# Second layer of a decoder trunk: a projection's weight splits tied behind the softmax scalings, and the last output rows' splits placed ahead of the begun rows' low parts

## The chip, the cores and the metric

The kernel runs on one core of a Trainium2 chip. The metric is the device time of one execution in microseconds (us), and the median of several runs is compared. The engines of a core work side by side, each through its own queue in order: TensorE (PE in the profile, with its weight loads as PEld), VectorE (DVE), ScalarE (ACT), GpSimd (POOL), and SyncE (SP), which here only issues DMA transfers.

## The reference

The model is a trunk of two layers over 512 tokens of width 1024, in float32. Only the second layer matters here. Before it, the first layer (a gated-DeltaNet mixer) and its feed-forward part have left the residual `x`. The second layer computes

```python
h = rms_norm(x, ln_mix[1])
proj = h @ swa_w_q                       # 12 query heads of 64, and 4 memory heads of 64
q = apply_partial_rope(proj[..., :768])
mix_out = sliding_window_attention(q, shared_k, shared_v, swa_sinks)   # window 128, 2 KV heads
mem_o = memory_attention(proj[..., 768:], mem_k, mem_v)                # 256 memory tokens
x = x + concatenate([mix_out, mem_o]) @ w_out[1]
x = x + swiglu(rms_norm(x, ln_ffn[1]), w_gate_up[1], w_down[1])
```

and the shared keys and values come from the normed `x` through `w_kv`. A final RMS norm follows.

## The kernel before, in words

Activations lie transposed: 128 channels on the partitions, 512 tokens along the free axis, so `x` is eight tiles `x[0..7]` of 128 x 512. Matrix products are made in a reduced format (fp32r) with a correction. Every operand is split in two: a high part, which is the value rounded to that format, and a low part, the rest. A product of a weight tile with an activation tile is three matmuls (`mm3`, L191): high times high, high times low, low times high. So a weight block of 128 x 1024 (one output tile of a projection, eight input tiles) costs 24 matmuls, and before them one split (`weight`, L180, with `split`, L166): an ACT copy `whi<-wraw` (L138) and a DVE subtraction `wlo<-wraw,whi` (L151). The raw block comes by one DMA of 512 KB (`load`, L174) into one of two `wraw` buffers. There are three pairs of `whi`/`wlo`, and two further pairs `oh`/`ol` for two output rows.

The attention part is `swa` (L1147). The queries are eight projections `queries(t)`: t = 0 to 5 are pairs of window heads, 6 and 7 the memory heads. For each tile t there follow

- `score(t)`: 16 matmuls into the PSUM tag `qk`, and DVE instructions that add the band mask and take the maxima (L751);
- `softmax(t)`: exponentials on ACT (L788), the denominators and their reciprocal on DVE (`den`, L793, L794), and the scaling of the exponentials by the reciprocal (`scale`, L799): for the token blocks n = 0 and 2 two instructions each on DVE (L806), for n = 1 and 3 two each on ACT (L804);
- `weighed(t)`: for each n, transposes of the scaled tile on PE into the PSUM tag `pt` (two banks), a copy out to `pf` (ACT L840, for n = 3 DVE L838), and then the products with the values, again into a `pt` bank;
- `settle(t)`: the result is split out of that bank into a high part (ACT, `h<-pt`) and a low part (DVE, `l<-pt,h`, L1213). The low part is kept behind the scaling that came last.

The tiles are taken in the order 6, 7, 0, 1, 2, 3, 4, 5. The loop at L1238 has steps t = 0 to 5: step t scores tile t, weighs the tile (6, 7, 0, 1, 2, 3)[t], softmaxes the tile (7, 0, 1, 2, 3, 4)[t], and in between, as PE work that needs nothing of these, runs the projection `queries(t + 2)` for t under 4 and the first four of eight input tiles of output row 0 or 1 for t = 4 and 5. After the loop tile 4 and tile 5 are weighed beside further pieces of the output rows 0 to 4. These five rows are generators (`row`, L866): each has its weight split when it starts, and they are "begun" with all input tiles but the last, tile 5.

`output` (L876) ends the projection. It finishes the begun rows 0 to 4 and makes the rows 5 to 7. For each row it adds the PSUM result to `x[m]` (L889), splits `x[m]` with the norm's gain into the next `h` and `l` for the feed-forward part (`split_gain`, L170, an ACT copy and a DVE `l<-x,gains,h` L154), and adds up squares. The weights of row m + 1 are asked for in turn m, and the update of `x[m]` is kept behind the low part of those weights (L890, L891).

The code gives the instructions in an order of emission, but the order on each engine is set by a planner at build time. It plays the program through with estimated costs, and gives each engine the instruction emitted first among those that it holds to be ready. `nosync(a, b)` (L114) tells it to keep `a` behind `b` on their engine, without any wait at run time. An instruction that was emitted late can thus stand early on its engine, if the planner saw a gap there. Once built, each queue runs strictly in the planner's order.

Further names that the steps use: `self.scaled` (the last DVE scaling), `self.copied` (the last ACT copy), `self.low` (the last low part), `self.loaded` (the last weight load; the feed-forward part's first transfers on SP are kept behind it), `token_sums` (L1015), which forms the sums `T` of activation tiles at the start of the feed-forward part.

Of the kernel before, what the change touches and what calls it, by code (L numbers as in the profile page):

```python
# [9 lines left out]
F32 = mybir.dt.float32  # L10
# [3 lines left out]
ALU = mybir.AluOpType  # L14
# [7 lines left out]
KD = D // P  # L22
# [63 lines left out]
class Builder:  # L86
    def __init__(self, tc, a):
        self.tc, self.nc, self.a = tc, tc.nc, a
        self.n = 0
        self.valued, self.turned, self.scaled, self.behind = None, [], None, None  # L90
        self.table, self.table_ins, self.table_users = None, None, []


# [17 lines left out]
    def bank(self, tag, shape=(P, T)):  # L111
        return self.t(self.pp, list(shape), F32, tag, self.pbufs[tag])
# [38 lines left out]
        return eng.tensor_tensor(out=out, in0=a, in1=b, op=op).ins  # L151

    def stt(self, out, in0, scalar, in1, op0, op1):
        self.nc.vector.scalar_tensor_tensor(out=out, in0=in0, scalar=scalar, in1=in1, op0=op0, op1=op1)  # L154

    def ts(self, out, in0, s1, op0, s2=None, op1=None):
        kw = {} if op1 is None else {"op1": op1}
# [11 lines left out]

    def split_gain(self, src, gain, hi, lo):  # L170
        self.copy(hi, src, scale=gain)
        self.stt(lo, src, gain, hi.bitcast(F32), ALU.mult, ALU.subtract)

    def load(self, src, pool=None, bufs=2):  # L174

# [1 line left out]
        self.loaded = self.nc.sync.dma_start(raw, src).ins  # L177
        return raw

    def weight(self, src, eng=None, raw=None, parts=1, pool=None, tags=("whi", "wlo"), bufs=3):  # L180

        raw = self.load(src) if raw is None else raw
        n = raw.shape[1]
        hi = self.t(pool or self.wpool, [P, D], F32R, tags[0], bufs)[:, :n]
        lo = self.t(pool or self.wpool, [P, D], F32R, tags[1], bufs)[:, :n]
        for i in range(parts):
            s = slice(i * n // parts, (i + 1) * n // parts)
            self.split(raw[:, s], hi[:, s], lo[:, s], eng or self.weng)
        return hi, lo

    def mm3(self, ps, w, k, act, start, stop, more=False):  # L191
# [585 lines left out]
    def softmax(self, scores, win):  # L777


        nc = self.nc  # L780
        sm, es, den, nm = scores
        if win:
            first = self.fn(es, es, AF.Exp)
            for n in range(NC):
                c0 = 0 if n else P
                for b in range(2):
                    i = b * NC + n
                    ins = self.fn(sm[n][:, b, c0:], sm[n][:, b, c0:], AF.Exp, scale=0.125, bias=nm[:, i:i + 1],  # L788
                                  accum_out=den[:, i:i + 1])
                    self.nosync(ins, first)  # L790
                    if self.turned:
                        self.nosync(ins, self.turned[n > 1 or n + b > 1])
            self.tt(nc.vector, den, den, es, ALU.add)  # L793
        nc.vector.reciprocal(den, den)  # L794
        if "pt" in self.pbufs:
            for n in range(NC):
                self.scale(sm, den, n, win)

    def scale(self, sm, den, n, win):  # L799
        p = sm[n][:, :, P if win and n == 0 else 0:]  # L800
# [62 lines left out]
            self.split(o, *out)  # L863


    def row(self, layer, m, mix, bank, w=None, **kw):  # L866

        w = self.weight(self.a["wout"][layer, m], **kw) if w is None else w
        for n, k in enumerate((6, 7, 0, 1, 2, 3, 4, 5)):
            if n:  # L870
                yield
            ps = bank() if n == 0 else ps
            self.mm3(ps, w, k, mix[k], n == 0, n == KD - 1)
        yield ps

    def output(self, xp, layer, mix, begun=()):  # L876

        nc, a = self.nc, self.a
        self.weng = nc.vector
        h = []  # L880
        self.acc = None
        hpool = self.apool if layer else self.bpool
        bank = lambda m: self.bank(("pj", "pj", "pt" if begun else "g")[m % 3])
        w = None
        for m in range(KD):
            ps = list(begun[m] if m < len(begun) else self.row(layer, m, mix, lambda: bank(m), w))[-1]
            ahead = bool(begun) and len(begun) <= m + 1 < KD
            w = self.weight(a["wout"][layer, m + 1]) if ahead else None
            self.ended = nc.vector.tensor_tensor(out=self.x[m], in0=ps, in1=self.x[m], op=ALU.add).ins  # L889
            if ahead:  # L890
                self.nosync(self.ended, self.low)  # L891
            hl = self.pair(hpool)
            self.split_gain(self.x[m], self.gain(G_FFN[layer], m), *hl)
            h.append(hl)
            self.acc = self.accumulate(xp, self.acc, self.x[m], m)
        self.behind = self.loaded if layer else None
        return h
# [249 lines left out]
    def swa(self, sp):  # L1147
        nc, a = self.nc, self.a
        memK, memV = self.fetch(sp, "mk"), self.fetch(sp, "mv")
        hk, h, qs, mix = [], [], {}, {}  # L1150
# [4 lines left out]
        sinks = self.small[:, 12:24].rearrange("p (b t) -> p t b", b=2)  # L1155
        kk, vv = [], []

        def queries(t):
            w = self.weight(a["wq"][t])
            ps = self.bank("pj")  # L1160
            for k in range(KD):
                self.mm3(ps, w, k, h[k], k == 0, k == KD - 1)
# [54 lines left out]
        def half():  # L1217
            if not free:
                two = self.bank("qk", [P, 2, 2, 2 * P])
                free.extend(two[:, i].rearrange("p a b -> p (a b)") for i in range(2))  # L1220
            return free.pop(0)

        rows = [self.row(1, m, mix, (lambda: self.bank("pj")) if m < 2 else half,
                         **(dict(pool=sp, tags=("oh", "ol"), bufs=2) if m > 2 else {})) for m in range(5)]
        some = lambda work, n: (next(work) for _ in range(n))
        got = {}
        for t in (6, 7):
            list(queries(t))
# [111 lines left out]
```

## Time and profile before

| | |
|---|---|
| median of the runs | 1169.27 us (1168.04, 1169.27 and 1171.07) |
| the profiled execution | 1167.55 us, of which the span from first to last instruction is 1165.7 |
| mean granted PE clock | 0.996 |
| attention of the second layer with the output projection | about 656 to 809 us of the span |

The low parts of the weights on DVE, in their order in the trace (start, us), with the weights that they belong to by the order of the loads:

| weights | low part starts | weights | low part starts |
|---|---|---|---|
| query tile 2 | 683.10 | output row 2 | 740.79 |
| query tile 3 | 694.76 | output row 4 | 742.64 |
| query tile 4 | 700.81 | output row 5 | 785.93 |
| query tile 5 | 706.42 | output row 6 | 796.26 |
| output row 0 | 717.57 | output row 7 | 798.00 |
| output row 1 | 728.92 | | |
| output row 3 | 735.06 | | |

How to read the views: times on a line are the start, from the beginning of the span, and the duration. An operation reads `out<-in` with the program's names, and `L151` is the line of the kernel or of its helper, so most subtractions are L151 and most ACT copies L138, and one goes by the names. Brackets hold the engine's idle time ahead of the instruction and what ended it. The scores of the steps 1 to 4 of the loop begin on PE at 706.4, 717.4, 728.6 and 739.9 us.

### The profile page before, as it was taken

What the parts mean: (1) busy time and instruction counts of PE and PEld (TensorE: products, weight loads), DVE (VectorE), ACT (ScalarE), POOL (GpSimd) and SP (SyncE); (2) the same over time, 40 slices, a digit from 0 to 9 for tenths busy, and PEclk for the clock granted to TensorE, in tenths of its full rate; (3) what the DMA queues carried; (4) which work ended last, traced back from release to release, by engine and by line L of the source; (5) the groups of instructions that cost most, each with busy time, mean ns of one, the idle gap of its engine ahead of it and who ended that gap; (6) DMA issues with size and microseconds to landing.
All of it is one profiled execution on the core that took longest, in us unless ns stands there. A gap on an engine that the chain in (4) does not pass through costs nothing.

```text
span 1165.7 us, 19273 instructions
## 1 busy us (share of the span) xinstructions
PE 1141.0 (98%) x7330; PEld 996.0 (85%) x7330; DVE 833.6 (72%) x1558; ACT 629.2 (54%) x1250; POOL 82.8 (7%) x93
## 2 busy tenths in 40 slices
PE   7999999999999999999999999998999999999996
PEld 6888778877899998899988877786899988999986
DVE  6654877767788876488956777828988734889654
ACT  7579572366466642266643556855666422566433
POOL 0210000000101101011100000001011000111000
PEclk9999999999999999999999999999999999999998
DMA  8434441324657736377633421206487633676232
GB/s 307 125 111 114 132 118 65 95 87 163 182 131 175 174 104 173 113 167 183 152 86 90 138 73 55 73 1 181 118 190 186 153 98 106 166 182 163 76 100 84
DMA packets 72943, 151.20 MB, mean 130 GB/s; under 512 B 16732, under 2 KB 19444, under 8 KB 72852
## 3 DMA queue, kind: packets, MB, share of 16 engines
q1 hardware_dynamic: 61908, 130.06, 36.6%
q0 software_dynamic: 10944, 19.93, 11.0%
q8 instruction: 57, 0.93, 0.3%
q14 instruction: 34, 0.28, 0.1%
HBM read 143.00 MB, written 6.96 MB: 129 GB/s over the span
## 4 chain that ended last, share of the span: by engine, by line
PE 90%; DVE 5%; ACT 2%; DMA 2%; issue 1%; SPq 0%; DVEq 0%; ACTq 0%
PE pj L144 43%; PE g L144 38%; PE sc L144 5%; PE qk L144 2%; PE pt L148 1%; DVE wlo L151 1%; PE pt L144 1%; DMA wraw<-in_wout 1%; DVE big L151 1%; PE g L148 1%; ACT sm L132 1%; DVE btmp L151 1%; DMA wraw<-in_wmk 1%; DVE qv L154 1%; ACT whi L138 0%
## 5 line engine op out<-in xcount | busy, mean ns | idle before, releaser
L138 ACT ACTIVATE whi<-wraw 128x512 fp32r<-128x512 f32 (+3 forms) x323 | 240.9, 752 | 262.8 <-PE pj L144 166.4
L151 DVE TENSOR_TENSOR wlo<-wraw,whi 128x512 fp32r<-128x512 f32 (+3 forms) x323 | 269.2, 842 | 103.5 <-ACT whi L138 98.1
L144 PE MATMUL pj<-h,wlo 128*128 128x512 f32 (+1 forms) x660 | 258.1, 391 | 3.7 <-DVE wlo L151 3.6
L144 PE MATMUL pj<-h,whi 128*128 128x512 f32 (+1 forms) x660 | 260.9, 396 | 0.1
L144 PE MATMUL pj<-l,whi 128*128 128x512 f32 (+1 forms) x660 | 259.0, 392 | 0.0
L144 PE MATMUL g<-T,whi 128*128 128x256 f32 x1216 | 220.6, 282 | 0.1
L144 PEld LDWEIGHTS g<-T,whi 128*128 128x128 f32 x1216 | 187.0, 189 | 1.4 <-DVE fu L154 1.1
L144 PE MATMUL g<-T,wlo 128*128 128x256 f32 x608 | 171.1, 281 | 0.0
L144 PEld LDWEIGHTS pj<-h,wlo 128*128 128x128 f32 x660 | 124.4, 189 | 29.4 <-DVE wlo L151 4.5
L144 PEld LDWEIGHTS pj<-h,whi 128*128 128x128 f32 x660 | 124.4, 189 | 29.0 <-issue 4.4
L144 PE MATMUL g<-h,whi 128*128 128x256 f32 (+1 forms) x500 | 146.6, 293 | 0.0
L144 PEld LDWEIGHTS pj<-l,whi 128*128 128x128 f32 x660 | 124.4, 188 | 25.2 <-issue 0.9
L144 PE MATMUL g<-h,wlo 128*128 128x256 f32 (+1 forms) x500 | 145.8, 292 | 0.0
L144 PE MATMUL g<-l,whi 128*128 128x256 f32 (+1 forms) x500 | 145.5, 291 | 0.0
L144 PEld LDWEIGHTS g<-T,wlo 128*128 128x128 f32 x608 | 114.4, 188 | 0.0
L144 PEld LDWEIGHTS g<-h,whi 128*128 128x128 f32 x500 | 94.9, 190 | 2.3 <-issue 0.5
L144 PEld LDWEIGHTS g<-l,whi 128*128 128x128 f32 x500 | 94.9, 190 | 2.3 <-issue 0.5
L144 PEld LDWEIGHTS g<-h,wlo 128*128 128x128 f32 x500 | 95.0, 190 | 1.7
L1053 POOL DMA_DIRECT2D ws<-in_wgu x38 | 33.0, 870 | 746.9 <-ACT h L138 245.0
L138 ACT ACTIVATE whi<-ws 128x512 fp32r<-128x512 f32 x76 | 48.0, 631 | 49.0 <-PE g L144 41.3
L151 DVE TENSOR_TENSOR fu<-pj,rstd 128x512 f32<-128x512 f32 (+1 forms) x34 | 22.4, 660 | 54.2 <-PE pj L144 54.2
L151 DVE TENSOR_TENSOR wlo<-ws,whi 128x512 fp32r<-128x512 f32 x76 | 52.1, 686 | 7.3 <-ACT whi L138 7.2
(375 smaller groups left out, 1679.7 us busy)
## 6 DMA issues: line engine op xcount, KB each, us to landing
wraw<-in_wgu SPq DMA_DIRECT2D x50, 512.0 KB, 4.2
ws<-in_wgu SPq DMA_DIRECT2D x76, 256.0 KB, 3.7
ws<-in_wgu POOLq DMA_DIRECT2D x76, 256.0 KB, 4.9
wraw<-in_win SPq DMA_DIRECT2D x26, 512.0 KB, 3.7
wraw<-in_wdn SPq DMA_DIRECT2D x32, 384.0 KB, 3.1
wraw<-in_wdn SPq DMA_DIRECT2D x32, 320.0 KB, 2.9
wraw<-in_wgu SPq DMA_DIRECT2D x38, 256.0 KB, 4.6
wraw<-in_wout SPq DMA_DIRECT2D x16, 512.0 KB, 3.6
```

Source lines behind the costliest of these rows:

```text
L132: ins = self.nc.scalar.activation(out, in_, func, **kw).ins
L138: self.copied = self.nc.scalar.activation(out, in_, AF.Copy, **kw).ins
L144: return self.nc.tensor.matmul(out, lhsT, rhs, start=start, stop=stop, skip_group_check=more).ins
L148: return self.nc.tensor.transpose(out, in_, self.ident[:k, :k]).ins
L151: return eng.tensor_tensor(out=out, in0=a, in1=b, op=op).ins
L154: self.nc.vector.scalar_tensor_tensor(out=out, in0=in0, scalar=scalar, in1=in1, op0=op0, op1=op1)
L1053: nc.gpsimd.dma_start(s1, a22, accum_op=ALU.add)
```

## The change

Two things are changed, both in the second layer.

First, `softmax` notes for each tile its last ACT scaling and its last DVE scaling in a list `scalings`, in the order 6, 7, 0, 1, 2, 3, 4, 5. `weight` takes a pair `after`: the high part is kept behind the first on ACT, the low part behind the second on DVE. The projection that runs in step s of the loop is given entry s - 1 of the list, the scalings of the tile that was weighed a step before: query tile 3 those of tile 6, query tile 4 those of tile 7, query tile 5 those of tile 0, output row 0 those of tile 1, row 1 those of tile 2. Row 2 gets those of tile 3, rows 3 and 4 those of tile 4.

Second, `output` first takes out the last matmuls of the begun rows, then asks for the weights of rows 5 and 6, and only then adds the rows to `x` one after the other; row 7's weights are asked for after the addition of row 4. The additions are no longer kept behind low parts of weights. Instead the low part of `x[0]` is kept behind the low part of row 6's weights.

For the first layer, which calls `output` with no begun rows, the program stays as it was. No instruction of the engines is added or taken away.

```diff
     def stt(self, out, in0, scalar, in1, op0, op1):
-        self.nc.vector.scalar_tensor_tensor(out=out, in0=in0, scalar=scalar, in1=in1, op0=op0, op1=op1)
+        return self.nc.vector.scalar_tensor_tensor(out=out, in0=in0, scalar=scalar, in1=in1, op0=op0, op1=op1).ins
...
         self.copy(hi, src, scale=gain)
-        self.stt(lo, src, gain, hi.bitcast(F32), ALU.mult, ALU.subtract)
+        self.low = self.stt(lo, src, gain, hi.bitcast(F32), ALU.mult, ALU.subtract)
...
-    def weight(self, src, eng=None, raw=None, parts=1, pool=None, tags=("whi", "wlo"), bufs=3):
+    def weight(self, src, eng=None, raw=None, parts=1, pool=None, tags=("whi", "wlo"), bufs=3, after=None):
...
             self.split(raw[:, s], hi[:, s], lo[:, s], eng or self.weng)
+            if after is not None:
+                self.nosync(self.copied, after[0])
+                self.nosync(self.low, after[1])
...
             for n in range(NC):
                 self.scale(sm, den, n, win)
+            self.scalings.append((self.copied, self.scaled))
...
-    def row(self, layer, m, mix, bank, w=None, **kw):
-
-        w = self.weight(self.a["wout"][layer, m], **kw) if w is None else w
+    def row(self, layer, m, mix, bank, w=None, after=None, **kw):
+
+        w = self.weight(self.a["wout"][layer, m], after=after and after(), **kw) if w is None else w
...
-        w = None
+        n, ws, lows = len(begun), [], []
+
+        def ahead(m):
+            if begun and n <= m < KD:
+                ws.append(self.weight(a["wout"][layer, m]))
+                lows.append(self.low)
+
+        done = [list(row)[-1] for row in begun]
+        for i in range(2):
+            ahead(n + i)
         for m in range(KD):
-            ps = list(begun[m] if m < len(begun) else self.row(layer, m, mix, lambda: bank(m), w))[-1]
-            ahead = bool(begun) and len(begun) <= m + 1 < KD
-            w = self.weight(a["wout"][layer, m + 1]) if ahead else None
-            self.ended = nc.vector.tensor_tensor(out=self.x[m], in0=ps, in1=self.x[m], op=ALU.add).ins
-            if ahead:
-                self.nosync(self.ended, self.low)
+            ps = done[m] if m < n else list(
+                self.row(layer, m, mix, lambda: bank(m), ws.pop(0) if ws else None))[-1]
+            self.ended = self.tt(nc.vector, self.x[m], ps, self.x[m], ALU.add)
+            if m >= n - 1:
+                ahead(m + 3)
             hl = self.pair(hpool)
             self.split_gain(self.x[m], self.gain(G_FFN[layer], m), *hl)
+            if m == 0 and lows:
+                self.nosync(self.low, lows[-1])
...
+        def behind(step):
+
+            return self.scalings[step - 1] if step > 0 else None
+
         def queries(t):
-            w = self.weight(a["wq"][t])
+            w = self.weight(a["wq"][t], after=behind(t - 2) if t < 6 else None)
...
+        own = dict(pool=sp, tags=("oh", "ol"), bufs=2)
         rows = [self.row(1, m, mix, (lambda: self.bank("pj")) if m < 2 else half,
-                         **(dict(pool=sp, tags=("oh", "ol"), bufs=2) if m > 2 else {})) for m in range(5)]
+                         after=lambda m=m: behind(min(m + 4, 7)), **(own if m > 2 else {})) for m in range(5)]
```

More of the change, by code (lines that the diff above doesn't have):

```diff
@@ L90, in __init__ @@
         self.valued, self.turned, self.scaled, self.behind = None, [], None, None
+        self.scalings = []
         self.table, self.table_ins, self.table_users = None, None, []
```

## The prediction

> **What bounds the kernel now.** First the page's head and the busy times.
>
> ```profile
> span 1165.7 us, 19273 instructions
> PE 1141.0 (98%) x7330; PEld 996.0 (85%) x7330; DVE 833.6 (72%) x1558; ACT 629.2 (54%) x1250; POOL 82.8 (7%) x93
> ```
>
> TensorE (PE) is busy for 98% of the span, so a change that adds no matmul and removes none can only win where PE stands still. PE's groups in the second layer's mixer and output projection (640 to 830 us) say how much that is; these two are the only ones with idle time before them (busy us, mean ns | idle us and releasers):
>
> ```profile
> L144 PE MATMUL pj<-h,wlo 128*128 128x512 f32 x149 | 58.9, 396 | 3.6 <-DVE wlo L151 3.6
> L148 PE MATMUL pt<-consts,sm 128*128 128x128 f32 x116 | 16.3, 274 | 2.4 <-DVE sm L806 1.6 <-ACT sm L138 0.5 <-DVE l L1213 0.3
> ```
>
> PE's instructions in order of time give the places (start, duration, in brackets the idle time before and its releaser):
>
> ```profile
> 721.30 0.63 PE L148 MATMUL pt<-consts,sm 128*128 128x128 f32 x4 [0.28 <-DVE l L1213]
> ...
> 732.64 0.63 PE L148 MATMUL pt<-consts,sm 128*128 128x128 f32 x4 [0.47 <-ACT sm L138]
> ...
> 741.64 0.50 PE L144 MATMUL pj<-h,whi 128*128 128x512 f32 x1
> ...
> 744.16 0.43 PE L148 MATMUL pt<-consts,sm 128*128 128x128 f32 x2 [1.55 <-DVE sm L806]
> ...
> 797.53 0.79 PE L144 MATMUL pj<-h,wlo 128*128 128x512 f32 x1 [3.64 <-DVE wlo L151]
> ```
>
> Three precede the transposes of a softmax tile (tiles 0, 1, 2, in steps 2, 3, 4 of the attention loop). The fourth stands in output row 6. It costs more than its length, as stretches of time show (length, PE, PEld, DVE, ACT, POOL busy, granted clock, DMA share, GB/s):
>
> ```profile
> 782.00:793.50 11.50, 11.50 (x52) 9.17 (x50) 8.20 (x12) 7.29 (x11) 0.33 (x1) 1.00 0.45 144
> 793.50:797.53 4.03, 0.39 (x2) 0.00 (x0) 3.80 (x6) 1.85 (x4) 3.18 (x4) 0.96 0.98 221
> 797.53:800.66 3.13, 3.12 (x7) 2.48 (x8) 3.13 (x6) 1.24 (x2) 0.00 (x0) 0.51 0.98 154
> ```
>
> After the wait the granted clock is 0.51 for 3.13 us, and seven matmuls take that time. At 11.50 / 52 = 0.22 us each they would take 1.55. The row-6 wait thus costs 3.64 + 1.6 = 5.2 us. The front waits leave the clock at 1.00 (rows below) and cost 0.28 + 0.47 + 1.55 = 2.30.
>
> **Part one: splits tied behind scalings.** A weight split is one ACT copy (whi) and one DVE subtraction (wlo). DVE's order before the three late transposes:
>
> ```profile
> 717.57 1.23 DVE L151 TENSOR_TENSOR wlo<-wraw,whi 128x1024 fp32r<-128x1024 f32 x1
> 718.71 0.69 DVE L151 TENSOR_TENSOR q<-q,rs 128x512 f32<-128x512 f32 x1
> ...
> 719.55 1.01 DVE L806 TENSOR_SCALAR sm<-sm,den 128x128 f32<-128x128 f32 x4
> ...
> 728.92 1.22 DVE L151 TENSOR_TENSOR wlo<-wraw,whi 128x1024 fp32r<-128x1024 f32 x1
> ...
> 730.88 1.01 DVE L806 TENSOR_SCALAR sm<-sm,den 128x128 f32<-128x128 f32 x4
> ...
> 740.79 1.23 DVE L151 TENSOR_TENSOR wlo<-wraw,whi 128x1024 fp32r<-128x1024 f32 x1 [0.44 <-ACT whi L138]
> ...
> 742.64 1.18 DVE L151 TENSOR_TENSOR ol<-wraw,oh 128x1024 fp32r<-128x1024 f32 x1
> 743.73 1.00 DVE L806 TENSOR_SCALAR sm<-sm,den 128x128 f32<-128x128 f32 x4
> ```
>
> These are the low parts of output rows 0, 1, 2 and 4. Each stands between a tile's exponentials and its scaling, though its row begins a step or more later. The change ties row 0 behind the scalings of tile 1, row 1 behind tile 2, row 2 behind tile 3, rows 3 and 4 behind tile 4, and query tile 5 behind tile 0. Query tiles 3 and 4 already stand behind theirs. No instruction is added or removed.
>
> Step 2 sheds 718.71 - 717.57 = 1.14 us of DVE time against a wait of 0.28. Step 3 sheds the same against 0.47. Step 4 sheds 0.44 + 1.14 + 1.09 = 2.67 against 1.55. All three waits should go: 2.30 us. The moved splits aren't late for their users: row 0's would start at about 732 (730.88 + 1.01), and its first matmul is the one at 741.64.
>
> **What that costs.** The copies move on ACT too, from in front of a scaling to behind it, where the copies out of the transposes (pf) follow at once:
>
> ```profile
> 739.71 1.04 ACT L138 ACTIVATE whi<-wraw 128x1024 fp32r<-128x1024 f32 x1
> 740.66 1.04 ACT L138 ACTIVATE oh<-wraw 128x1024 fp32r<-128x1024 f32 x1
> ...
> 742.82 1.71 ACT L138 ACTIVATE sm<-sm,den 128x256 f32<-128x256 f32 x4 [0.64 <-DVE den L794]
> 744.63 0.39 ACT L138 ACTIVATE pf<-pt 128x256 f32<-128x256 f32 x1
> 745.77 1.09 ACT L138 ACTIVATE pf<-pt 128x512 f32<-128x512 f32 x2 [0.76 <-PE pt L148]
> ```
> ```profile
> 740.00:750.00 10.00, 8.42 (x72) 6.34 (x74) 8.39 (x31) 8.51 (x25) 0.00 (x0) 1.00 0.35 107
> 750.00:760.00 10.00, 9.96 (x80) 7.89 (x81) 7.22 (x34) 9.71 (x34) 0.00 (x0) 1.00 0.00 0
> ```
>
> Between 740 and 760 ACT is idle for only 1.49 + 0.29 = 1.78 us. In that stretch two copies go (rows 2 and 4) and two come (rows 1 and 2), so ACT's work stays, and tile 4's scaling can come forward by 1.78 at most where PE comes forward by 2.30. I charge the difference, 0.5. The bounds: 0, if PE fills the gap with row matmuls (its order holds some there), and 2.3, if ACT reclaims none of its idle time. I stay near the low end, because 0.64 + 0.76 of the idle time waits for DVE's late denominators and PE's late transposes, the things that move. Tile 5 has room in any case:
>
> ```profile
> 766.95 1.70 ACT L138 ACTIVATE sm<-sm,den 128x256 f32<-128x256 f32 x4
> ```
> ```profile
> 772.71 0.82 PE L148 MATMUL pt<-consts,sm 128*128 128x128 f32 x6
> ```
>
> Its scaling ends 4 us before its transposes, which covers the copies of rows 3 and 4 that now fall into that stretch. If that cover were gone, they would cost 2 x 0.95 = 1.9 (start to start, 739.71 to 740.66).
>
> The loads (SP's queue) come later too, since a raw buffer is free only when the second split before it is done. Row 2's load waits for row 0's low part (about 733) and has until tile 3's scaling, a step after tile 2's at 743.73; the later ones have similar room. The FFN's transfers queue behind row 7's load at 787.17 (below) as before. I cost this at nothing, with the projections' own matmuls as the cover; the last rival prices it without.
>
> **Part two: the end of the projection.** The chain of row 6:
>
> ```profile
> 784.41 2.01 ACT L138 ACTIVATE whi<-wraw 128x1024 fp32r<-128x1024 f32 x2 [2.13 <-PE pj L144]
> ...
> 792.02 1.06 ACT L138 ACTIVATE whi<-wraw 128x1024 fp32r<-128x1024 f32 x1 [1.67 <-DMA wraw<-in_wout]
> ```
> ```profile
> 785.93 1.22 DVE L151 TENSOR_TENSOR wlo<-wraw,whi 128x1024 fp32r<-128x1024 f32 x1
> ...
> 793.73 0.75 DVE L154 SCALAR_TENSOR_TENSOR l<-x,gains,h 128x512 fp32r<-128x512 f32 x1 [1.58 <-ACT h L138]
> ...
> 796.26 1.22 DVE L151 TENSOR_TENSOR wlo<-wraw,whi 128x1024 fp32r<-128x1024 f32 x1
> ```
> ```profile
> 787.17 4.77 DMA wraw<-in_wout
> ```
>
> Row 6's high part has been ready since 786.4 (the second of the two copies). Its low part runs at 796.26, behind low parts of the begun rows (l) that wait for ACT, which itself stands for row 7's load with those rows' h queued behind it. The change emits the splits of rows 5 and 6 ahead of the begun rows' updates and puts the low part of x0 behind row 6's. That low part then follows row 5's, near 787 to 788, and PE wants it at 793.9. The cost is 1.14 us of delay for x0's l, whose user is the FFN's first projection, behind row 7 (798.3 + 24 x 0.22 = 803.6). The wait and the slow clock go: 5.2 us. Late next is row 7. Its load still starts when row 5's low part ends (787.15) and lands at 791.94, its copy ends at 793.1, and PE, at 793.9 four matmuls into row 6's 24, reaches row 7 at 793.9 + 20 x 0.22 = 798.3. That is 5 us for one subtraction of 1.22.
>
> The rule in the Trainium skill, "TensorE: Matmul & The Clock Gate" (Part 1), is that the clock is halved after an idle window of about 3.4 us that runs freely. By it a wait of 3.64 need not cover a whole window in every execution; where it doesn't, the row-6 term is 3.64, not 5.2. In this trace the clock did fall.
>
> **Sum.** 2.30 - 0.5 + 5.2 = 7.0. The profiled execution took 1167.55 us (span 1165.7 and 1.85 around it), so 1160.55. The median shown is 1169.27, 1.72 above it: 1162.3. What a measurement can't tell from no change is 0.3%, 3.5 us.
>
> **The rivals.**
>
> *The slow clock isn't in the timed runs* (the rule above as a mechanism): the idle time is only just long enough here, since the clock over 793.50 to 797.53 averages 0.96 and so fell near the end of the wait. Then the gain is 7.0 - 1.6 = 5.4, and 1163.9. The one trace speaks against it. Chance 0.12.
>
> *ACT keeps the front's gain*: the new whi behind the scaling delays pf and the next exponentials, and tile 4's transposes come no earlier. For it: ACT's 9.71 of 10 us. Against it: the same number of copies in the stretch. Gain 5.2, 1164.1. Chance 0.08.
>
> *The tail's gain is given back at the FFN's opening*, where DVE is dense:
>
> ```profile
> 820.00:830.00 10.00, 10.00 (x46) 8.29 (x45) 9.47 (x18) 6.82 (x10) 0.00 (x0) 1.00 0.13 46
> ```
> ```profile
> 829.09 1.21 DVE L151 TENSOR_TENSOR T<-raw,T 128x1024 fp32r<-128x1024 f32 x1
> ```
> ```profile
> 833.15 0.40 PE L144 MATMUL g<-T,whi 128*128 128x256 f32 x2
> ```
>
> The last token sum is ready at 830.3 and used at 833.15, 2.9 us of room. If DVE doesn't come forward at all, PE waits for the rest, 7.0 - 2.9 = 4.1: gain 2.9, and 1166.4. Against it: the row-6 wait held DVE as well, and what it waits for there (x5 to x7) comes earlier. Chance 0.12.
>
> *The order doesn't turn out as the change says*: the planner finds new places for everything, the gaps are filled by other splits, and row 7 inherits row 6's wait. Gain 0 to 2, 1168. Chance 0.08.
>
> *Slower*: with later splits the ring of two raw buffers turns later, and a copy whose load hasn't landed stands at the head of ACT with the scalings and pf behind it. The load in the chain above took 4.77 us. It decides when the split two before ends less than that ahead of the scaling. If that holds for rows 2, 3 and 4, PE waits three times 4.77, and each wait is longer than the 3.64 that brought the slow clock: 3 x (4.77 + 1.6) = 19.1 less 7.0, so 12 us slower, 1181. Against it: row 0's low part (733) ends over 10 us ahead of tile 3's scaling. Chance 0.06.
>
> **How the numbers follow.** The forecast as summed has the remaining 0.54. Its own range is gains of 5.3 (ACT's upper bound, 2.3 in place of 0.5, and a little of the FFN's waits) to 9 (the runs differ by some 1.5 around their median): 1160 to 1164. Adding the first three rivals carries the range to 1167 and its content to about 0.8. Faster by over 0.3% are the forecast and the first two rivals, 0.74. The FFN rival and the unchanged order lie within 0.3%: 0.20. Slower: 0.06.
>
> **What would show it.** Right: no wlo or ol between the exponentials and the scalings of tiles 0 to 2, no PE wait above 0.3 before their transposes; row 6's wlo before 790, ahead of every l of the begun rows; granted clock 1.00 from 782 to 810; the same DVE busy time. Wrong: a PE wait of a microsecond or more on pf or sm in steps 4 and 5, on row 7's whi or wlo, or on T or h after 800; a PE clock below 1 in the mixer.

## The result, and the profile after

The changed kernel takes 1162.9 us (median; 1161.25 to 1163.84), the kernel before 1168.8 beside it (1167.56 to 1171.07). The ratio is 0.9946, with an interval of 0.9932 to 0.9961: about 6 us faster. The forecast was 1162.3 and a gain of 7.0.

The head of the profile's page of the changed kernel, and below it PE's groups from 640 to 860 us that have idle time before them (busy us, mean ns | idle us and releasers):

```profile
span 1162.0 us, 19272 instructions
...
PE 1141.1 (98%) x7330; PEld 995.3 (86%) x7330; DVE 833.6 (72%) x1558; ACT 628.4 (54%) x1250; POOL 82.9 (7%) x93
```
```profile
L145 PE MATMUL pj<-h,whi 128*128 128x512 f32 x155 | 63.1, 407 | 0.2 <-ACT h L139 0.2
L145 PE MATMUL pj<-l,whi 128*128 128x512 f32 x155 | 60.9, 393 | 0.3 <-DVE l L155 0.3
L145 PE MATMUL g<-T,whi 128*128 128x256 f32 x98 | 17.9, 282 | 0.9 <-ACT fs L139 0.9
```

(The changed kernel's lines count a few more: L145 is the matmul that was L144, L139 the copy that was L138, L152 the subtraction that was L151, L155 the low part that was L154.) The 2.4 us before the transposes and the 3.6 us in row 6 are gone. In their place stand three short waits, all behind row 7: at the end of the feed-forward part's first projection and before its product with `T`. The busy times are the same, as they should be.

VectorE's order in the front, at tile 2's scaling (start, duration):

```profile
742.21 1.01 DVE L811 TENSOR_SCALAR sm<-sm,den 128x128 f32<-128x128 f32 x4
746.22 1.22 DVE L152 TENSOR_TENSOR wlo<-wraw,whi 128x1024 fp32r<-128x1024 f32 x1
```

Row 1's subtraction follows tile 2's scaling by 3 us; rows 0 and 2 stand in the same way behind tiles 1 and 3. At the end of the projection, first VectorE's rows and then ScalarE's:

```profile
785.71 2.35 DVE L152 TENSOR_TENSOR wlo<-wraw,whi 128x1024 fp32r<-128x1024 f32 x2
787.98 1.41 DVE L155 SCALAR_TENSOR_TENSOR l<-x,gains,h 128x512 fp32r<-128x512 f32 x2
...
793.05 1.23 DVE L152 TENSOR_TENSOR wlo<-wraw,whi 128x1024 fp32r<-128x1024 f32 x1 [1.26 <-ACT whi L139]
```
```profile
791.95 1.06 ACT L139 ACTIVATE whi<-wraw 128x1024 fp32r<-128x1024 f32 x1 [3.48 <-DMA wraw<-in_wout]
```

Rows 5 and 6 have their low parts by 788.06, ahead of every `l` of the begun rows. Row 7's comes at 793.05, after ScalarE has stood 3.48 us for its load; TensorE doesn't feel that. Stretches of time (length, PE, PEld, DVE, ACT, POOL busy, granted clock, DMA share, GB/s), the first two those of the prediction:

```profile
793.50:797.53 4.03, 4.03 (x19) 3.33 (x19) 4.03 (x7) 3.87 (x7) 2.15 (x3) 1.00 0.87 269
797.53:800.66 3.13, 3.13 (x16) 2.58 (x15) 3.13 (x5) 1.93 (x3) 0.47 (x1) 1.00 0.93 228
750.00:760.00 10.00, 10.00 (x77) 7.46 (x73) 8.31 (x35) 10.00 (x31) 0.00 (x0) 1.00 0.22 69
...
800.00:810.00 10.00, 9.48 (x41) 7.11 (x40) 8.14 (x16) 5.43 (x8) 0.86 (x1) 1.00 0.85 212
810.00:820.00 10.00, 10.00 (x43) 7.92 (x44) 10.00 (x18) 6.34 (x8) 0.00 (x0) 1.00 0.34 107
820.00:830.00 10.00, 10.00 (x57) 8.75 (x55) 9.85 (x17) 5.61 (x10) 0.86 (x1) 1.00 0.10 26
```

The clock stays at 1.00. ScalarE is full from 750 to 760, and VectorE from 810 to 830. What is lost anew lies at the opening of the feed-forward part. The instructions of three engines there, in order of time:

```profile
804.87 0.68 DVE L152 TENSOR_TENSOR x<-pj,x 128x512 f32<-128x512 f32 x1
...
806.74 1.06 ACT L139 ACTIVATE whi<-wraw 128x1024 fp32r<-128x1024 f32 x1 [3.76 <-DMA wraw<-in_wgu]
...
807.71 0.71 ACT L139 ACTIVATE h<-x,gains 128x512 fp32r<-128x512 f32 x1
...
808.45 0.75 DVE L155 SCALAR_TENSOR_TENSOR l<-x,gains,h 128x512 fp32r<-128x512 f32 x1 [1.71 <-ACT h L139]
808.47 0.50 PE L145 MATMUL pj<-h,whi 128*128 128x512 f32 x1 [0.24 <-ACT h L139]
```

`x[7]` is complete at 805.55, but ScalarE stands 3.76 us for the weights of the feed-forward part's gate tile 1, with the `h` of `x[7]` queued behind their copy. So `h` ends at 808.42, VectorE waits 1.71 us for it and TensorE twice, 0.24 us for `h` and 0.28 for `l`. VectorE then has work without a gap for 20 us, and the lateness comes out at the end of it:

```profile
828.56 0.63 ACT L139 ACTIVATE whi<-wraw 128x512 fp32r<-128x512 f32 x1 [1.84 <-DVE wraw L152]
...
830.66 0.36 ACT L139 ACTIVATE fs<-g 128x256 f32<-128x256 f32 x1
```
```profile
831.08 0.50 PE L145 MATMUL g<-T,whi 128*128 128x256 f32 x2 [0.87 <-ACT fs L139]
```

ScalarE waits for a sum of weights from VectorE, and the copy that frees TensorE's bank (`fs<-g`) stands behind it in ScalarE's queue.

**Four marks.** The profiled executions differ by up to 2.7 us before the change's first effect: score 1, the first matmul of step 1, began at 706.35 us in the profile before and between 706.4 and 709.1 in the others, whatever the kernel. So I compare profiles from that mark on, by three stretches: to the first transposes of tile 5, to the feed-forward part's first sum of squares (`g<-sqa`), and to the end of the span. The rows of the three marks in the profile of the changed kernel:

```profile
708.59 1.79 PE L145 MATMUL qk<-ks,q 64*128 64x128 f32 x16
...
772.48 0.82 PE L149 MATMUL pt<-consts,sm 128*128 128x128 f32 x6
...
809.85 1.12 PE L145 MATMUL g<-sqa,consts 128*128 128x512 f32 x2
```

All profiles, in us (each number is a difference of two such rows, or of the span and the last; the kernels of the experiments are described below):

| kernel | score 1 to tile 5 | tile 5 to sum of squares | to the end | all |
|---|---|---|---|---|
| before, three profiles | 66.36, 66.20, 66.35 | 41.81, 43.16, 42.81 | 351.2, 351.0, 350.9 | 459.3, 460.3, 460.1 |
| part one alone, two profiles | 63.90, 63.88 | 42.83, 42.85 | 351.0, 350.9 | 457.7, 457.7 |
| part two alone | 66.39 | 37.29 | 352.2 | 455.9 |
| changed, three profiles | 63.89, 63.89, 63.89 | 37.37, 37.03, 37.12 | 352.2, 352.2, 352.3 | 453.4, 453.1, 453.3 |
| changed, ScalarE's copies doubled | 65.74 | 36.62 | 352.2 | 454.5 |
| changed, gate 1's split tied back | 63.90 | 36.29 | 352.0 | 452.2 |
| changed, row 7's own buffer | 63.88 | 36.27 | 350.8 | 450.9 |
| both | 63.89 | 36.27 | 350.7 | 450.8 |

The change gains 2.4 in the front and 5.4 in the tail, and gives 1.2 back in the feed-forward part: 6.6 by the means of the profiles, 6 by the medians of the runs. The shortest second column is 36.27, in the two kernels without any wait of TensorE there; I take it as the floor. So the kernel before lost 5.5 to 6.9 us there, and the changed kernel still loses 0.8 to 1.1.

### The profile page after: what moved, and what is told of

Same layout as the page of the kernel before. It is cut to its first block, busy times and chain, and to the rows that moved or that the text cites. A ratio compares the mean times of both kernels' runs of the same rounds, so it can differ in the third digit from the quotient of the medians.

```text
span 1162.0 us, 19272 instructions
## 1 busy us (share of the span) xinstructions
PE 1141.1 (98%) x7330; PEld 995.3 (86%) x7330; DVE 833.6 (72%) x1558; ACT 628.4 (54%) x1250; POOL 82.9 (7%) x93
## 4 chain that ended last, share of the span: by engine, by line
PE 91%; DVE 4%; ACT 2%; DMA 2%; issue 1%; SPq 0%; DVEq 0%; ACTq 0%
PE pj L145 43%; PE g L145 38%; PE sc L145 5%; PE qk L145 2%; PE pt L149 1%; PE pt L145 1%; DVE wlo L152 1%; DVE big L152 1%; PE g L149 1%; DVE btmp L152 1%; DMA wraw<-in_wmk 1%; DMA wraw<-in_wgu 1%; DVE qv L155 1%; ACT whi L139 0%; DMA wraw<-in_wout 0%
## 5 line engine op out<-in xcount | busy, mean ns | idle before, releaser
L139 ACT ACTIVATE whi<-wraw 128x512 fp32r<-128x512 f32 (+3 forms) x323 | 241.1, 752 | 260.5 <-PE pj L145 153.3
L152 DVE TENSOR_TENSOR wlo<-wraw,whi 128x512 fp32r<-128x512 f32 (+3 forms) x323 | 269.6, 843 | 101.8 <-ACT whi L139 96.3
L145 PE MATMUL pj<-h,whi 128*128 128x512 f32 (+1 forms) x660 | 261.2, 397 | 0.4 <-ACT h L139 0.2
L145 PE MATMUL pj<-l,whi 128*128 128x512 f32 (+1 forms) x660 | 259.0, 392 | 0.3 <-DVE l L155 0.3
L145 PE MATMUL pj<-h,wlo 128*128 128x512 f32 (+1 forms) x660 | 257.7, 391 | 0.0
L145 PE MATMUL g<-T,whi 128*128 128x256 f32 x1216 | 220.6, 282 | 0.9 <-ACT fs L139 0.9
L145 PEld LDWEIGHTS g<-T,whi 128*128 128x128 f32 x1216 | 186.9, 189 | 2.2 <-DVE fu L155 1.1
L145 PE MATMUL g<-T,wlo 128*128 128x256 f32 x608 | 171.1, 281 | 0.0
L145 PEld LDWEIGHTS pj<-h,whi 128*128 128x128 f32 x660 | 124.2, 188 | 29.8 <-issue 4.4
L145 PEld LDWEIGHTS pj<-l,whi 128*128 128x128 f32 x660 | 124.4, 188 | 25.9 <-issue 0.9
L145 PE MATMUL g<-h,whi 128*128 128x256 f32 (+1 forms) x500 | 146.5, 293 | 0.0
L145 PEld LDWEIGHTS pj<-h,wlo 128*128 128x128 f32 x660 | 124.2, 188 | 25.3 <-DVE wlo L152 0.4
L145 PE MATMUL g<-h,wlo 128*128 128x256 f32 (+1 forms) x500 | 145.8, 292 | 0.0
L145 PE MATMUL g<-l,whi 128*128 128x256 f32 (+1 forms) x500 | 145.5, 291 | 0.0
L145 PEld LDWEIGHTS g<-T,wlo 128*128 128x128 f32 x608 | 114.4, 188 | 0.0
L145 PEld LDWEIGHTS g<-h,whi 128*128 128x128 f32 x500 | 95.0, 190 | 2.3 <-issue 0.5
L145 PEld LDWEIGHTS g<-l,whi 128*128 128x128 f32 x500 | 94.9, 190 | 2.3 <-issue 0.5
L145 PEld LDWEIGHTS g<-h,wlo 128*128 128x128 f32 x500 | 95.0, 190 | 1.8
L139 ACT ACTIVATE whi<-ws 128x512 fp32r<-128x512 f32 x76 | 48.0, 631 | 48.8 <-PE g L145 41.0
L152 DVE TENSOR_TENSOR fu<-pj,rstd 128x512 f32<-128x512 f32 (+1 forms) x34 | 22.4, 660 | 54.3 <-PE pj L145 54.1
L152 DVE TENSOR_TENSOR wlo<-ws,whi 128x512 fp32r<-128x512 f32 x76 | 52.1, 686 | 7.3 <-ACT whi L139 7.2
```

Of the source, the lines that this page charges most:

```text
L139: self.copied = self.nc.scalar.activation(out, in_, AF.Copy, **kw).ins
L145: return self.nc.tensor.matmul(out, lhsT, rhs, start=start, stop=stop, skip_group_check=more).ins
```

## The experiments

Theory: the two parts act apart, each by the wait that it removes, and what is given back comes of gate 1's late load on ScalarE. The main rivals: the parts need each other; ScalarE's full stretch takes something of the front's gain; and VectorE's fullness alone makes the loss in the feed-forward part. The ratios are to the kernel before, run beside each on the same chip: 1168.8 us for the parts, the tie and the changed kernel with them, 1168.7 for the buffer, both, the doubled copies and the changed kernel with those.

### Part one alone

The ties of the splits stay; the projection's end is that of the kernel before.

```diff
+            self.ended = nc.vector.tensor_tensor(out=self.x[m], in0=ps, in1=self.x[m], op=ALU.add).ins
+            if ahead:
+                self.nosync(self.ended, self.low)
```

> Part one alone: the splits are tied behind the scalings, and the end of the projection is the old one. Theory A (the three front waits go and nothing takes their place): 2.3 to 2.5 us faster than before, no PE wait in the attention steps, and the 3.6 us wait in row 6 unchanged, with the granted clock near half speed for about 3 us behind it. Theory B (ACT is full there and keeps a part): 1.8 us or less, with a PE wait on a copy or a scaling in steps 4 to 6. If the slow clock behind the row-6 wait depends on chance, it is missing in some of the profiles.

Measured: 1167.1 us (1165.96 to 1168.04), ratio 0.9984 (0.9975 to 0.9993), 1.7 us faster. The time alone would fit theory B (1.8 us or less), but the wait that goes with it isn't there: in the front the profile has no wait of TensorE, and the stretch is 2.4 us shorter, as theory A has it. By the marks the whole is 2.2 us shorter. The row-6 wait is the only one left, 3.39 us in place of 3.64, but the slow clock behind it (granted clock in the last column but two) lasts longer than in the profile before:

```profile
794.86 0.80 PE L145 MATMUL pj<-h,wlo 128*128 128x512 f32 x1 [3.39 <-DVE wlo L152]
```
```profile
791.49:794.86 3.37, 0.00 (x0) 0.00 (x0) 3.37 (x6) 1.19 (x3) 2.52 (x3) 0.85 0.96 193
794.86:800.70 5.84, 5.84 (x14) 4.59 (x15) 4.56 (x9) 1.24 (x2) 0.00 (x0) 0.50 1.01 220
```

Fourteen matmuls at half the clock against seven. Whether that belongs to part one is the question of the last experiment.

### Part two alone

The new `output` stays; the ties are left out, of the query tiles and the rows alike.

```diff
             self.split(raw[:, s], hi[:, s], lo[:, s], eng or self.weng)
-            if after is not None:
-                self.nosync(self.copied, after[0])
-                self.nosync(self.low, after[1])
```

> Part two alone: rows 5 and 6 are split ahead, the ties behind the scalings are left out. Theory A (the row-6 wait and its slow clock are worth 5.2, and about 1.6 of it is given back at the opening of the feed-forward part): 3.5 to 3.9 us faster than before, the three front waits (0.28, 0.47, 1.55) unchanged, and PE waits on h, l and fs between 800 and 835. Theory B (nothing is given back, the missing microsecond is the front's): 5.2 us faster.

Measured: 1165.5 us (1164.64 to 1165.87), ratio 0.9967 (0.9955 to 0.9979), 3.4 us faster, near theory A's 3.5 to 3.9 and far from theory B's 5.2. PE's groups with idle time, 640 to 860 us:

```profile
L145 PE MATMUL pj<-l,whi 128*128 128x512 f32 x153 | 60.2, 393 | 0.3 <-DVE l L155 0.3
L145 PE MATMUL g<-T,whi 128*128 128x256 f32 x94 | 17.2, 283 | 0.8 <-ACT fs L139 0.8
L149 PE MATMUL pt<-consts,sm 128*128 128x128 f32 x116 | 16.4, 275 | 2.4 <-DVE sm L808 1.6 <-ACT sm L139 0.5 <-DVE l L1229 0.3
```

The front's three waits are back unchanged, and the row-6 wait is gone. The two waits at the feed-forward part's opening are there without part one, so they belong to part two. The parts act apart: in the table part one shortens the first column alone and part two the second. By the medians 1.7 and 3.4 make 5.1 of the 6 us; the rest is within the spread of the runs and of the slow clock's length.

### Gate 1's split tied behind the last row's parts

The changed kernel, with the split of gate tile 1's weights kept behind the `h` and `l` of `x[7]`.

```diff
+        self.final_split = (self.copied, self.low)
         return h
...
-            ps = self.project(col(f, 0), h, "pj")
+            w = self.weight(col(f, 0), after=self.final_split) if layer and f == 1 else None
+            ps = self.project(col(f, 0), h, "pj", w=w)
```

> The changed kernel, and the high part of the feed-forward part's third weight block (gate tile 1) kept behind the last row's h on ACT. Theory A (what is given back at the opening comes from ACT standing 3.8 us for that block's load with the last h behind it): the PE waits on h and l near 808 go, DVE's idle 1.7 us there too, and with them most of the 0.9 us on fs: 1.0 to 1.6 us faster than the changed kernel, 7 to 7.5 faster than before. Theory B (DVE is the bound of the opening, whoever stands in ACT's queue): at most 0.4 faster than the changed kernel, and the wait on fs grows.

Measured: 1160.4 us (1160.16 to 1160.98), ratio 0.9925 (0.9913 to 0.9937). That is 2.4 us below the changed kernel run beside it. By the marks, against the mean of the changed kernel's three profiles, the tie is worth 1.06: 0.88 in the second column, which comes to its floor, and 0.18 behind it. The other 1.4 us of the medians are more than the profiles show, and I can't place them. One PE wait is left:

```profile
828.22 0.51 PE L145 MATMUL g<-T,whi 128*128 128x256 f32 x2 [0.78 <-ACT fs L139]
```

So `h` being queued behind the late load made the waits on `h` and `l`. Theory A also had most of the wait before the product with `T` go, and there it was wrong: setting `h` ahead of the load doesn't remove that one. The changed kernel itself, beside it:

> The changed kernel once more, for comparison on the same chip: 5.5 to 6.3 us faster than before by every theory. If the first layer's clock loss of the first profile (0.90 between 200 and 210 us) depends on chance, it is missing or elsewhere in this profile.

It took 1162.85 us (1161.8 to 1163.84), ratio 0.9945 (0.9932 to 0.9957), as in the first comparison. The clock loss in the first layer is missing in this profile and in the third. In the first profile it is this stretch, in which TensorE is busy throughout:

```profile
198.65:202.07 3.42, 3.42 (x23) 2.32 (x23) 1.70 (x6) 0.69 (x1) 0.00 (x0) 0.50 0.52 156
```

By half its length it delays score 1 by an estimated 1.7 us, and score 1 begins at 708.59 us there against 706.91 in this profile.

### Row 7's own buffer

Row 7's raw weights are loaded into a buffer of their own (the one in which the memory tiles' transposed weights stood, free since those tiles were weighed), in place of the two buffers in turn. The order of ScalarE keeps gate 1's split ahead of `h`, but the loads of row 7 and of the feed-forward part's first two weight blocks (gate 0 and up 0) don't wait for low parts any more.

```diff
-                ws.append(self.weight(a["wout"][layer, m]))
+                raw = None
+                if m == KD - 1:
+                    raw = self.t(self.sp, [P, 2, 2, T], F32, "pfm", 1).rearrange("p a b t -> p (a b t)")[:, :D]
+                    self.loaded = nc.sync.dma_start(raw, a["wout"][layer, m]).ins
+                ws.append(self.weight(a["wout"][layer, m], raw=raw))
```

> The changed kernel with row 7's raw weights in a buffer of their own, and no tie on gate tile 1's split: ScalarE's order stays as in the changed kernel, only the loads are earlier. Theory (the changed kernel lost about 0.9 us at the feed-forward part's opening because gate 1's load lands late while the last row's h is queued behind its split, and by how much varies from run to run): with the load landing some 5 us earlier ScalarE doesn't stand, the waits on h and l of the last row go as they did with the tie; 1160.0 to 1160.6 us and a spread under 1 us. Rival (the order of the split itself costs, 1 us of copy ahead of h, however early the load): 1162 to 1163 us, waits on h and l remain.

Measured: 1159.8 us (1159.77 to 1161.12), ratio 0.9925 (0.9913 to 0.9938). ScalarE's and VectorE's rows at the place:

```profile
802.91 0.69 DVE L152 TENSOR_TENSOR x<-pj,x 128x512 f32<-128x512 f32 x1
...
805.05 0.75 DVE L155 SCALAR_TENSOR_TENSOR l<-x,gains,h 128x512 fp32r<-128x512 f32 x1 [0.27 <-ACT h L139]
```
```profile
803.35 1.06 ACT L139 ACTIVATE whi<-wraw 128x1024 fp32r<-128x1024 f32 x1 [2.36 <-DMA wraw<-in_wgu]
804.31 0.71 ACT L139 ACTIVATE h<-x,gains 128x512 fp32r<-128x512 f32 x1
```

The split still stands ahead of `h`, and still waits for its load, but the load lands at 803.35, before `x[7]` is complete at 803.60. The copy costs `h` 0.7 us and VectorE 0.27. From 640 to 860 us no PE group has idle time left. So the same order costs TensorE nothing when the load is early: the waits on `h` and `l` took the order and the lateness together, and taking away either removes them. Gate 1's load itself still follows a low part, gate 0's: counted from score 1 it is issued at 89.9 us against 91.3 in the changed kernel, and its copy begins at 95.4 against 98.2. The time is just under the theory's range, and the spread of 1.35 us over the theory's 1. The third column falls from 352.2 to 350.8, to what it was before the change: the wait before the product with `T` is gone too. The first low part of a token sum on VectorE behind `x[7]` (`T<-raw,T`) begins at 806.52 us here and at 809.91 in the changed kernel. Counted from score 1 (708.00 and 708.59) that is 98.5 and 101.3 us: VectorE is 2.8 us earlier there.

### Both together

The tie on gate 1's split and row 7's own buffer.

> The kernel with gate tile 1's split behind the last row's h and l (1160.4 us), and row 7's raw weights in a buffer of their own, the one in which the memory tiles' transposed weights had stood, so that row 7's load and the feed-forward part's first two loads no longer wait for the low parts of rows 5, 6 and 7. No work is added. Theory (what is left at the feed-forward part's opening is VectorE's work, delayed by ScalarE's standing for row 7's load, 3.4 us, behind which VectorE idles 1.2): that idle time goes, and so does most of the wait of 0.8 before the second product with T; 1159.6 us. Rival (VectorE is full from 805 to 820 whatever stands before, and the token sums wait for x5 to x7, not for VectorE's earlier time): the wait stays at 0.7 to 0.8, 1160.4 us. Second rival (the loads crowd each other: row 5's and 6's share the channels with row 7's and the gates'): a PE wait on row 1's to 6's high part, 1161 us or more.

Measured: 1160.9 us (1159.63 to 1161.22), ratio 0.993 (0.9917 to 0.9942). No PE group from 640 to 860 us has idle time. Two of the stretches:

```profile
810.00:820.00 10.00, 10.00 (x46) 8.29 (x45) 9.79 (x17) 7.15 (x11) 0.00 (x0) 1.00 0.28 102
820.00:830.00 10.00, 10.00 (x65) 9.10 (x64) 8.61 (x14) 6.37 (x12) 0.86 (x1) 1.00 0.43 101
```

By the marks it gains 1.4 us over the tie alone, where the theory expected 0.8, and nothing over the buffer alone; the median doesn't show this gain, and is 1.3 us above the theory's time. The rival that VectorE's fullness alone makes the last wait falls: from 810 to 820 us VectorE is nearly as full here (9.79 against 10.00), but it is earlier with its work, and the wait is gone. The wait on a high part that the second rival foresaw doesn't appear. The medians of these three variants, 1159.8 to 1160.9, don't tell them apart; all three are about 8 us faster than the kernel before and 2 to 3 faster than the changed one.

The changed kernel beside these two:

> The changed kernel again, for its spread beside the others on one chip. Theory: 1162.9 us, with a spread of 2 us or more that comes of when gate 1's load lands and of short stretches of lower clock in the first layer. Rival (the spread is the chip's and of the order of the day): the other kernels of this call spread as much.

It took 1162.85 us, with a spread of 0.4 us this time (1162.77 to 1163.20). The theory on its spread was wrong: ScalarE's wait for gate 1's load is 3.76, 3.77 and 3.92 us in its three profiles, so it doesn't vary. What varies is the stretch ahead of score 1: in the three profiles it ends at 708.59, 706.91 and 707.72 us, and what follows takes 453.4, 453.1 and 453.3.

### ScalarE's copies doubled

The high parts of rows 1 and 2 are copied twice (`twice=m in (1, 2)` where the rows are made). Nothing else is added.

```diff
+            if twice:
+                self.copy(hi[:, s], raw[:, s])
+                self.nosync(self.copied, after[0])
             self.split(raw[:, s], hi[:, s], lo[:, s], eng or self.weng)
```

> The changed kernel with the high parts of output rows 1 and 2 copied twice, both behind the scalings of tiles 2 and 3: two copies of 0.95 us more on ScalarE in the stretch in which it is busy for 10.0 of 10 us, and nothing else. Theory (ScalarE's full stretch is not on the path: TensorE has row and query matmuls to do meanwhile, so the prediction's term of 0.5 was nothing): within 0.5 us of the changed kernel, 1162.9. Rival (ScalarE is at its brink there, as the prediction's 0.5 had it: whatever is added delays pf, the exponentials and the transposes): 1 to 1.9 us slower than the changed kernel, 1164 to 1164.8, with PE waits on pf or sm in steps 4 and 5.

Measured: 1163.7 us (1163.1 to 1164.39), ratio 0.9955 (0.9942 to 0.9967), 0.8 above the changed kernel, between the theory's 0.5 and the rival's 1. Two waits on PE in the front:

```profile
744.63 1.14 PE L149 MATMUL pt<-consts,sm 128*128 128x128 f32 x8 [0.83 <-ACT pf L139]
...
753.85 1.15 PE L149 MATMUL pt<-consts,sm 128*128 128x128 f32 x8 [1.05 <-ACT pf L139]
```

Two copies of 0.95 us cost 0.83 + 1.05 = 1.88 us of waiting, and the front stretch grows by 1.85. Of it 0.4 to 0.7 comes back in the tail (36.62 against 37.0 to 37.4), which is why the whole grows by less; why the tail is shorter wasn't tried. So the rival was right on the mechanism: ScalarE is at its brink there. In the front these two copies were paid in full, and the copies of the changed kernel cost TensorE no wait.

### The length of the slow clock

The kernel before was profiled twice more, and part one alone once more, one execution each.

> The kernel before again, one look at the stretch of low clock behind the wait of 3.6 us in row 6. Theory (the clock's stretch is as long as it happens to fall, since it follows its own window and not the wait's end): the stretch lasts another time than the 3.1 us of the first look, anywhere from nothing to about 6 us. Rival (it belongs to the program: 3.1 us in the kernel before, 5.7 us with part one alone): 3.1 us again, within 0.4.

> As the look before it: by the theory a third length, by the rival 3.1 us again.

> Part one alone again, one look: by the theory the stretch of low clock behind the wait of 3.4 us lasts another time than the 5.7 us of the first look, by the rival 5.7 us again, within 0.4. Score 1 to the first matmul of tile 5's weighing takes 71.1 us by both.

The three took 1171.2, 1169.0 and 1167.5 us. The row-6 wait and the stretch from its end to the return of the clock, of the kernel before twice and of part one alone:

```profile
796.45:799.97 3.52, 0.00 (x0) 0.00 (x0) 3.52 (x6) 1.33 (x3) 2.65 (x3) 0.91 0.95 187
799.97:806.20 6.23, 6.23 (x15) 4.88 (x16) 4.55 (x9) 1.24 (x2) 0.00 (x0) 0.50 1.00 230
```
```profile
794.68:798.09 3.41, 0.00 (x0) 0.00 (x0) 3.41 (x6) 1.23 (x3) 2.54 (x3) 0.84 0.99 173
798.09:803.50 5.41, 5.41 (x13) 4.25 (x14) 4.55 (x9) 1.24 (x2) 0.00 (x0) 0.50 1.03 237
```
```profile
793.12:796.78 3.66, 0.00 (x0) 0.00 (x0) 3.66 (x6) 1.47 (x3) 2.80 (x4) 0.78 0.89 160
796.78:801.75 4.97, 4.97 (x12) 3.95 (x13) 4.56 (x9) 1.24 (x2) 0.00 (x0) 0.50 1.02 185
```

The same program gives 3.13, 6.23 and 5.41 us of slow matmuls, part one 5.84 and 4.97. The length doesn't belong to the program, as the theory had it; but in none of the five was it near nothing. The trace also holds the start and the length of each stretch at half clock, from inside the wait on: 3.41 us in the first profile of before, and 6.83 in the other four.

## Why the prediction was right, and where it wasn't

**Front, 2.30 predicted.** Right: 2.4 by the marks, in every profile with part one (but for the doubled copies, which put 1.85 back) and in none without it. All three waits went, by the order foreseen.

**ScalarE's charge, 0.5.** Wrong in size: nothing was lost. The step that failed is "tile 4's scaling can come forward by 1.78 at most where PE comes forward by 2.30". It took the idle time of one window of 20 us as the limit, but ScalarE enters that window earlier too. The scalings of tiles 2 and 4 of the changed kernel, and tile 4's of the kernel before:

```profile
742.27 1.71 ACT L139 ACTIVATE sm<-sm,den 128x256 f32<-128x256 f32 x4 [0.56 <-DVE den L798]
...
758.55 1.71 ACT L139 ACTIVATE sm<-sm,den 128x256 f32<-128x256 f32 x4
```
```profile
758.78 1.71 ACT L138 ACTIVATE sm<-sm,den 128x256 f32<-128x256 f32 x4
```

Counted from score 1, tile 2's begins at 33.68 us and not at 742.82 - 706.35 = 36.47, 2.8 earlier, and tile 4's at 49.96 and not at 52.43, 2.5 earlier. The mechanism behind the charge was real, as the doubled copies show: with two copies more, PE waits 1.88 us.

**Row 6, 3.64 + 1.6 = 5.2.** The wait went, the step was right. The clock's term was undersized: 1.6 was worked out from the mildest of five stretches. At half the clock a stretch costs half its length, so the five cost 1.6, 3.1, 2.7, 2.9 and 2.5, on the mean 2.6. By the marks the whole is 42.6 - 36.27 = 6.3 us on the mean of the three profiles of before, of which waits and slow clock explain 6.0.

**"Late next is row 7" with 5 us of room.** Right: its low part ended at 794.28, and no PE wait stands in row 7, though ScalarE stood 3.48 us for its load.

**"The FFN's transfers queue behind row 7's load ... as before. I cost this at nothing."** This is the step that failed. The transfers did not go as before: the load of gate 1's weights lands too late for its place in ScalarE's queue. Its issue comes forward, and by more than the work does, but then it takes nearly twice as long. In both kernels it is issued when gate 0's low part frees a buffer, in the changed one this:

```profile
798.61 1.22 DVE L152 TENSOR_TENSOR wlo<-wraw,whi 128x1024 fp32r<-128x1024 f32 x1
```

The load itself (count, KB each, us from issue to landing), and the stretch from its issue to its landing, first in the kernel before, with the addition that completes `x[7]` there, then in the changed one:

```profile
wraw<-in_wgu SPq DMA_DIRECT2D x1, 512.0 KB, 3.6
```
```profile
806.66:810.31 3.65, 3.65 (x18) 3.03 (x17) 3.65 (x6) 1.50 (x3) 0.00 (x0) 1.00 0.62 159
```
```profile
809.94 0.68 DVE L889 TENSOR_TENSOR x<-pj,x 128x512 f32<-128x512 f32 x1
```
```profile
wraw<-in_wgu SPq DMA_DIRECT2D x1, 512.0 KB, 6.7
```
```profile
799.91:806.66 6.75, 6.75 (x31) 5.62 (x30) 6.71 (x13) 2.26 (x4) 0.86 (x1) 1.00 1.09 248
```

Counted from score 1, `x[7]` is complete at 104.3 us before and at 97.0 after, 7.3 earlier, and the load is issued at 100.3 and 91.3, 9.0 earlier. But it lands at 104.0 and 98.1: 0.3 ahead of `x[7]` before, and 1.1 behind it after. The price by the marks: 0.8 to 1.1 us at the rows' end, and 1.2 before the product with `T`, 2.0 to 2.3 in all. The third rival had named the place and priced 4.1 by VectorE's fullness; the cause was a load that ScalarE stood for, and VectorE's fullness only carried the delay on. Its statement "if DVE doesn't come forward at all" was too strong: VectorE's last token sum came forward by 5.3 of the 7.8 us that TensorE had gained by then (829.09 and 826.04, counted from score 1).

**The sum.** 2.4 + 6.3 - 0.9 - 1.2 = 6.6 against 7.0. So the nearness of the forecast is in part luck: row 6's term was 1.1 too small and the front's 0.6, and the give-back of 2.1, which wasn't in it, made up for them.

**The first rival, no slow clock in the timed runs.** It falls as far as five profiles can say: each of them has it. The Trainium skill's rule ("TensorE: Matmul & The Clock Gate", Part 1) of a window that runs freely fits the lengths: the time at half clock, counting the part of the wait that the granted clock of its row gives (for the second profile of before 2 x 0.09 x 3.52 = 0.6), is 3.5, 6.9, 6.5, 6.9 and 6.6 us. That is one or two windows of the page's 3.4, and the lengths in the traces, 3.41 and four times 6.83, agree. I had drawn the wrong conclusion from it, that the clock might not fall: in all five it fell, and what varied was whether it stayed low for one window or two.

**The slower rival** had nothing for it: no wait on a load appeared in front of a scaling.

## What to carry to other kernels

When a stall in front of a boundary goes, look at the loads that serve the work behind it: their landing need not move forward as far as the work, as here, where the load was issued 9.0 us earlier and landed 5.9 earlier. An in-order engine that stands for such a load holds everything queued behind it, so either the loads are freed earlier (here by a buffer of its own for one of them) or the urgent instruction is set ahead of the copy. By the marks the first took back 2.4 us, the second 1.1. Profiles of one kernel that start the changed part at different times are compared from a mark just ahead of it, and what one profile shows of the clock behind a wait is one draw, not the price.

## What the runs showed that was not expected

The clock fell before the wait had lasted 3.4 us. In the second profile of part one alone the granted clock over the 3.66 us of waiting is 0.78, so it stood at a half for 2 x 0.22 x 3.66 = 1.6 us of it: it fell about 2.1 us into the wait. In the third profile of before it is 0.84, which puts the fall 2.3 us in. Less than one window of 3.4 us without a matmul was thus enough. So a shorter wait than these may bring half clock too; no run here has one between 1.6 us, which left the clock alone in the front, and 3.4. Nor does half clock need a long wait at all: from 190 to 202 us of the changed kernel's first profile TensorE is busy throughout, and the clock still stood at a half from 198.65 to 202.07. What brought it there wasn't tried. The price of a wait of 3.4 to 3.7 us was 5.5 to 6.9 us in all.

A load of 512 KB isn't one price. Gate 1's took 3.6 us in the kernel before, at a DMA share of 0.62, and 6.7 in the changed one, issued 9.0 us earlier, at a share of 1.09. That the other loads in flight make the difference is likely, but no run changes them alone.
